# First layer's opening of a two-layer decoder trunk: row tiles side by side in fixed orders, products that nobody reads, and compression behind the first gates

## The chip, the cores and the metric

One Trainium2 chip, one core. The metric is device microseconds of one execution, median of several runs. The core has five engines that run their own instruction streams and wait for each other by semaphores: TensorE (PE, with its weight loads shown apart as PEld), VectorE (DVE), ScalarE (ACT), GpSimd (POOL) and SyncE (SP, which here issues the transfers from DRAM).

## The reference, cut to what matters

A sequence of 256 rows of width 1024 goes through two layers. Each layer normalises its rows, projects them, mixes them in two head groups (a gated linear recurrence and a block-sparse attention), and ends with a gated feed-forward block.

```
for l in range(DEPTH):                                  # 2 layers
    xn = rms_norm(h, norm_mix[l])                       # 256 x 1024
    proj = xn @ w_in[l]                                 # columns: hq hf hi hg | nq kc vc ksl vsl ksw vsw | gates
    o_hg = hgrn2_mixer(hq, hf, hi, hg, lb[l], hg_gnorm[l])
    o_nsa = nsa_mixer(nq, kc, vc, ksl, vsl, ksw, vsw, ngate, ...)
    h = h + concat(o_hg, o_nsa) @ w_out[l]
    xn = rms_norm(h, norm_ffn[l])
    h = h + (silu(g) * u) @ w_ffn_out[l]                # g, u = xn @ w_ffn_in[l]
# inside nsa_mixer: kc, vc = compress(...) = silu(blocks @ w1) @ w2, with w1 of 2048 x 256 for k and for v
```

## The kernel before

Rows are two tiles of 128 (t = 0, 1). Every float32 product is made of three: an operand is split into a high part (`whi`, `xh`; written by ScalarE as a copy in a shorter format) and a low part (`wlo`, `xl`; VectorE's difference), and `mm3` adds high·high, high·low and low·high in PSUM. So each weight piece ("unit", 512 KB, or 280 KB for the narrow block C) is loaded into one of 4 raw buffers (`wraw`), split by ScalarE (line 143) and VectorE (line 144) into one of 6 split buffers, and used by TensorE. A raw buffer is free when its unit is split; a split buffer is free when TensorE has used its unit for the last time.

The input projection runs in column blocks: B (4 units; keys and values of compression and of one attention branch), C (4 narrow units), A (4 units; the queries), then the gates: for the first pair of heads `hf` (2 units, PSUM tile `pf`) and `hq` (2 units, `pq`), later the same for the second pair. B, C and A are computed by `proj_tok` for row tile 0 over all four units and then for row tile 1, so a unit is held until row tile 1 has used it. `pf`, `pq` and the PSUM tiles of B and A (`pt`) share the two banks of tag "a" in turn: `pf` takes the bank in which A's row tile 0 stood.

Compression takes B's result: ScalarE copies it out (`kvc`, line 444), TensorE turns it (`pa`, line 458), VectorE writes `flat`; 64 narrow products with `w1` (8 loads of 512 KB, tile `w`, line 470) give `phid` (line 510), then `hid`, `phT`, `hk` and `hv`, `pkc`, and at last `kcb` and its transpose `pkT` (line 551).

A scheduler puts each engine's instructions in order when the program is built; on the chip each engine then takes its own list strictly in that order. `tc.high_priority` moves instructions ahead, and `after(a, b)` makes a stand behind b. Loads go out by SP's list in the same way. There are 8 transfer semaphores, used in turn, so SP issues a load only when the load 8 places earlier has landed.

The opening is `norm_T` for each row tile: squares (ScalarE), a power of -0.5 (GpSimd), scaling by the row's factor and the norm's weights (`xn`, VectorE, line 343), transposes (TensorE, line 346), and the split of the transposed rows (`x`, lines 351 and 352). The weights of the first norm are one row of 1024 numbers; `pgain` (line 250) spreads it over 128 partitions by a product with a row of ones.

Of the kernel before, what the change touches and what calls it, by code (L numbers as in the profile page):

```python
# [43 lines left out]
HOLD, HOLD_C = (18, 18, 16, 36), 1  # L44

# [45 lines left out]
def trunk(ctx: ExitStack, tc: tile.TileContext, x, w_in, w_out, lbl, gnorm, q_gain, k_gain,  # L91
# [19 lines left out]
    def unit(src, a, b):  # L111
        units.append([src, a, b, None, None, None, None])
        return len(units) - 1
# [19 lines left out]
    def split_to(n):  # L133
        while state["split"] < min(n, len(units)):
            load_to(state["split"] + 1)
            u = units[state["split"]]
            a, b = u[1], u[2]
            hi = wsp.tile([128, 1024], F32R, name="whi")
            lo = wsp.tile([128, 1024], F32R, name="wlo")
            u[4] = hi[:, : a * b].rearrange("p (a b) -> p a b", b=b)  # L140
            u[5] = lo[:, : a * b].rearrange("p (a b) -> p a b", b=b)
            with tc.high_priority(offset=SPLIT_PRIO):
                after(S.activation(u[4], u[3], AF.Copy), state.pop("behind", ()))  # L143
                u[6] = V.tensor_sub(u[5], u[3], u[4].bitcast(F32))  # L144
            state["split"] += 1
# [89 lines left out]
    ident = C("ident")  # L235
# [8 lines left out]
    nc.gpsimd.memset(mhalf, -0.5)  # L244
    ones = one.tile([128, 128], F32, name="ones")
    nc.gpsimd.memset(ones[0:1], 1.0)
# [11 lines left out]
    for hp in range(2):  # L258
        nc.gpsimd.memset(AT[hp], 0.0)

    kB = one.tile([128, 2, 2, T], F32R, name="kB")
    for g in range(2):
        nc.gpsimd.memset(kB[64 - 64 * g:128 - 64 * g, g].bitcast(F32), 0.0)
# [35 lines left out]
    def setup_tables():  # L299
        G = nc.gpsimd  # L300
        V.tensor_copy(idb, ident)
        V.tensor_copy(cab, tmp0[:, :128])
        V.tensor_copy(lev_m, tmp0[:, 128:208])
        for l in range(NL):
            gq = qk_g[:, 64 * l:64 * l + 64]
            ks = [qk_g[:, NL * 64 + 192 * l + 64 * b:NL * 64 + 192 * l + 64 * b + 64] for b in range(3)]
            for i, g in enumerate((gq, ks[1], ks[2])):
                gb = g[:, None, :].to_broadcast([128, NT, 64])
                G.tensor_mul(tabs[:, l, i, 0], cos, gb)
                for a in range(2):  # L310
                    s0, s1 = slice(32 * a, 32 * a + 32), slice(32 - 32 * a, 64 - 32 * a)
                    G.tensor_mul(tabs[:, l, i, 1, :, s0], sin[:, :, s0],
                                 g[:, None, s1].to_broadcast([128, NT, 32]))
                if i == 0:
                    G.tensor_scalar(tabs[:, l, i], tabs[:, l, i], 0.125, None, op0=OP.mult)
            G.tensor_mul(tabc[:32, l, 0], C("cosc", 32), ks[0][:32])
            for a in range(2):
                s0, s1 = slice(32 * a, 32 * a + 32), slice(32 - 32 * a, 64 - 32 * a)
                G.tensor_mul(tabc[:32, l, 1, s0], C("sinc", 32)[:, s0], ks[0][:32, s1])

# [8 lines left out]
    def norm_T(t, gain, xh, xl, tag, behind=(), hold=None):  # L329

        with tc.high_priority():
# [3 lines left out]
            for a in range(2):  # L335
                cs = slice(512 * a, 512 * a + 512)
                sq = S.activation(xn[:, cs], h[:, t, cs], AF.Square, scale=D ** -0.5, accum_out=ss[:, a:a + 1])
                after(sq, behind)
# [22 lines left out]
    for l in range(NL):  # L361
# [3 lines left out]
        last = [norm_T(0, gain0, *X[:2], "c", hold=end + HOLD[0] if l else None)[0]]  # L365
        if l == 0:
            norm_T(1, gain0, *X[:2], "c", last)
            setup_late()
            setup_tables()
# [69 lines left out]

        begin = len(products)  # L440
        for t, p in proj_tok("B"):
# [8 lines left out]

        flat = wk.tile([128, 2, 16, 32], F32, name="flat", tag="n4", bufs=3)
# [14 lines left out]
        w1t = []  # L466
        for u in range(4):
            w = wk.tile([128, 2, 4, 256], F32, name="w1", tag="big" if u < 3 else "turn", bufs=3 if u < 3 else 1)
            for i, w1 in enumerate((w1_k, w1_v)):
                DMA.dma_start(w[:, i], w1[l].rearrange("(j p) n -> p j n", p=128)[:, 4 * u:4 * u + 4])  # L470
            w1t.append(w)

# [25 lines left out]
        rs = rstd(ss, 24, 64, "qk_rs")  # L498
        gates(0)


        p = bank("phid", "e")[:, :256]
        for u in range(4):
# [539 lines left out]
```

## Time and profile before

| what | value |
|---|---|
| median of 3 runs | 684.99 us (684.43 to 685.22) |
| profiled execution, its own time | 685.0 us |
| its span (first to last instruction) | 683.1 us |
| TensorE busy | 667.0 us, 98% of the span |
| weight loads of TensorE busy | 554.6 us, 81% |
| VectorE busy | 469.7 us, 69% |
| ScalarE busy | 379.6 us, 56% |
| transfers | 118.9 MB, 174 GB/s on average |

Busy times of the engines overlap, so they don't add up. The time of an execution is 1.9 us more than its span. A share of TensorE near 100% says that it is seldom idle, not that it runs at its peak: a matmul that is slow counts as busy.

### The profile page before, as it was taken

Reading aid. Unit: us, or ns where it says so; the run is one execution under the profiler, and the core shown is the slowest. Engines: PE = TensorE matmul, PEld = TensorE weight load, DVE = VectorE, ACT = ScalarE, POOL = GpSimd, SP = SyncE. Lnnn points to the kernel's source line nnn. Section 1 sums busy time; section 2 is a strip of 40 time slices with the busy share of each in tenths; the row PEclk is TensorE's granted clock in tenths of the full one; section 3 lists DMA queues with packets and bytes.
Section 4 is the critical chain, followed back from the end, with each engine's and each line's share of the span. In section 5 each row is a group of like instructions: output and inputs, shape, how many; then the busy total and the mean of one; then the engine's idle time right before and its main releaser. Section 6 shows DMA issues by size and latency. Waiting matters only on the chain.

```text
span 683.1 us, 11845 instructions
## 1 busy us (share of the span) xinstructions
PE 667.0 (98%) x4607; PEld 554.6 (81%) x4607; DVE 469.7 (69%) x853; ACT 379.6 (56%) x676; POOL 30.1 (4%) x72
## 2 busy tenths in 40 slices
PE   6999999999999999999999999999999999999997
PEld 3869876688888888888878897658898888888886
DVE  4879999577665556666588979858685566665552
ACT  5536778636555555555466558656555555555550
POOL 2600001001000000000010000010000000000000
PEclk9999999999999999999999999999999999999999
DMA  7798541353765665666678632404376666665521
GB/s 253 246 335 266 169 107 51 100 178 121 248 187 187 190 192 194 194 185 185 196 230 286 203 110 64 125 1 154 94 229 203 188 187 190 197 191 187 185 93 62
DMA packets 86574, 118.90 MB, mean 174 GB/s; under 512 B 5035, under 2 KB 69365, under 8 KB 86518
## 3 DMA queue, kind: packets, MB, share of 16 engines
q1 hardware_dynamic: 86518, 118.15, 56.1%
q8 instruction: 36, 0.59, 0.4%
q14 instruction: 20, 0.16, 0.1%
HBM read 117.08 MB, written 1.05 MB: 173 GB/s over the span
## 4 chain that ended last, share of the span: by engine, by line
PE 80%; DVE 8%; DMA 4%; ACT 4%; issue 2%; POOL 1%; SPq 0%; POOLq 0%; DVEq 0%; ACTq 0%
PE pgu L929 22%; PE pz L327 17%; PE pgu L932 11%; PE pt L327 9%; PE py L327 5%; DMA wraw<-in_w_in_dram 4%; DVE wlo L144 3%; PE pO L673 2%; PE pgt L327 2%; ACT whi L143 2%; PE pPT L662 2%; PE pf L327 1%; PE pxn L346 1%; PE pl L779 1%; PE pq L327 1%
## 5 line engine op out<-in xcount | busy, mean ns | idle before, releaser
L144 DVE TENSOR_TENSOR wlo<-wraw,whi 128x1024 fp32r<-128x1024 f32 (+1 forms) x204 | 244.9, 1206 | 141.7 <-ACT whi L143 140.6
L143 ACT ACTIVATE whi<-wraw 128x1024 fp32r<-128x1024 f32 (+1 forms) x204 | 212.4, 1044 | 147.1 <-PE pgu L929 43.5
L929 PE MATMUL pgu<-x,whi 128*128 128x512 f32 x640 | 174.7, 394 | 0.0
L929 PEld LDWEIGHTS pgu<-x,whi 128*128 128x128 f32 x640 | 110.7, 189 | 15.7
L327 PE MATMUL pz<-whi,ahl 128*128 128x512 f32 x352 | 112.5, 391 | 0.0
L932 PEld LDWEIGHTS pgu<-x,wlo 128*128 128x128 f32 x640 | 98.1, 189 | 13.5
L932 PE MATMUL pgu<-x,wlo 128*128 128x256 f32 x640 | 101.7, 281 | 0.0
L327 PE MATMUL pt<-whi,x 128*128 128x512 f32 (+1 forms) x320 | 97.9, 383 | 0.0
L327 PEld LDWEIGHTS pz<-whi,ahl 128*128 128x128 f32 x352 | 65.9, 188 | 13.9 <-DVE ahl L946 0.5
L327 PE MATMUL pz<-wlo,ahl 128*128 128x512 f32 x176 | 68.9, 392 | 0.0
L327 PEld LDWEIGHTS pt<-whi,x 128*128 128x128 f32 x320 | 58.5, 191 | 10.3 <-DVE x L352 0.5
L327 PE MATMUL pt<-wlo,x 128*128 128x512 f32 (+1 forms) x160 | 61.6, 385 | 0.3 <-DVE wlo L144 0.3
L327 PE MATMUL py<-whi,x 128*128 128x512 f32 x128 | 42.0, 398 | 0.0
L327 PEld LDWEIGHTS pz<-wlo,ahl 128*128 128x128 f32 x176 | 33.0, 188 | 6.4
L327 PEld LDWEIGHTS pt<-wlo,x 128*128 128x128 f32 x160 | 30.6, 191 | 5.2 <-DVE wlo L144 0.7
L592 ACT ACTIVATE P<-pS,nm 128x128 f32<-128x128 f32 (+1 forms) x64 | 26.1, 424 | 6.3 <-DVE nm L639 5.0
L327 PEld LDWEIGHTS py<-whi,x 128*128 128x128 f32 x128 | 24.1, 188 | 4.7
L938 ACT ACTIVATE sl<-sl 128x512 f32<-128x512 f32 x20 | 12.7, 634 | 27.0 <-DVE sl L937 27.0
L327 PE MATMUL py<-wlo,x 128*128 128x512 f32 x64 | 25.1, 392 | 0.0
L327 PE MATMUL pf<-x,whi 128*128 128x256 f32 x128 | 23.8, 286 | 0.1
L327 PE MATMUL pgt<-whi,x 128*128 128x256 f32 x128 | 23.8, 285 | 0.0
L327 PE MATMUL pq<-x,whi 128*128 128x256 f32 x128 | 23.6, 284 | 0.0
(222 smaller groups left out, 829.4 us busy)
## 6 DMA issues: line engine op xcount, KB each, us to landing
wraw<-in_w_ffn_in_dram SPq DMA_DIRECT2D x88, 512.0 KB, 3.6
wraw<-in_w_in_dram SPq DMA_DIRECT2D x48, 512.0 KB, 5.3
wraw<-in_w_ffn_out_dram SPq DMA_DIRECT2D x44, 512.0 KB, 3.7
w<-in_cmp_w_k_dram SPq DMA_DIRECT2D x8, 512.0 KB, 4.7
w<-in_cmp_w_v_dram SPq DMA_DIRECT2D x8, 512.0 KB, 7.1
wraw<-in_w_out_dram SPq DMA_DIRECT2D x16, 256.0 KB, 4.1
wraw<-in_w_out_dram SPq DMA_DIRECT2D x8, 512.0 KB, 4.9
wraw<-in_w_in_dram SPq DMA_DIRECT2D x8, 280.0 KB, 5.3
```

The source lines that it names most:

```text
L143: after(S.activation(u[4], u[3], AF.Copy), state.pop("behind", ()))
L144: u[6] = V.tensor_sub(u[5], u[3], u[4].bitcast(F32))
L327: products.append(PE.matmul(o, a[u], b[v], start=start and i == 0, stop=stop and i == 2, skip_group_check=skip))
L346: tr = PE.transpose(p[:, 128 * k:128 * k + 128], xn[:, 512 * c + 128 * k:512 * c + 128 * k + 128], ident)
L592: e = S.activation(o, i, f, **kw)
L662: PE.transpose(p[:, 128 * hg:128 * hg + 128], P[t, g][:, hg, b, 128 * sb:128 * sb + 128], ident)
L673: m = PE.matmul(po[64 * g:64 * g + 64], vtok[:, b, sb, 64 * g:64 * g + 64], pts[g][0], start=(b == 0 and sb == 0), stop=False, skip_group_ ...
L779: m = PE.matmul(pl[32 * n:32 * n + 32, hp, 2 * t + i], K[:, i, ts], QF[:, i, ts].rearrange("p (n c a) -> p n c a", c=2, a=half)[:, :, 1], ...
L929: products.append(PE.matmul(pp[b], w[0][:, k, s], X[2][:, 4 * hh + k].rearrange("p c t -> p (c t)"), start=(hh == 0 and k == 0), stop=Fals ...
L932: products.append(PE.matmul(pp[b][:, T:], w[1][:, k, s], X[0][:, 4 * hh + k], start=False, stop=(hh == 1 and k == 3), skip_group_check=True))
L938: S.activation(sl, sl, AF.Silu)
```

## The change

The first layer's opening is written out by hand in `first_rows`, with the order of ScalarE, VectorE and GpSimd fixed by `after`. Block B of the first layer is computed by `proj_first`, with the two row tiles side by side unit by unit. The norm's weights go by ScalarE's queue into a row of a zeroed tile and are spread by products of 128 rows (`first` is a matrix with ones in its first row only). The identity matrix is made by GpSimd in place of a load. Seven bf16 products of 512 columns (`spin`), which nobody reads, stand at the head of TensorE's list. GpSimd's memsets and tables come behind the norms. The loads of `w1` and the products with it stand behind the first gates in the program, and `setup_late` and three casts stand later.

```diff
+SPIN = 7
     grow = wk.tile([128, D], F32, name="gain")
-    DMA.dma_start(grow[0:1], norm_mix[0:1])
+    cst = one.tile([128, NKEEP], F32, name="cst")
+    idle = one.tile([128, 512], BF16, name="idle")
+    V.memset(idle, 1.0)
+    V.memset(grow[:, :512], 0.0)
+    G.memset(ident, 1.0)
+    G.memset(grow[:, 512:], 0.0)
+    G.affine_select(ident, ident, pattern=[[-1, 128]], compare_op=OP.is_equal, fill=0.0, base=0, channel_multiplier=1)
...
+    last_pool = G.memset(first[0:1], 1.0)
+    S.dma_start(grow[0:1], norm_mix[0:1])
...
-    cst = one.tile([128, NKEEP], F32, name="cst")
-    DMA.dma_start(cst[:, :128], consts[:, :128])
...
+    def spin(n):
+        for _ in range(n):
+            PE.matmul(spin_bank, idle[:, :128], idle, start=True, stop=True)
+
+    spin(SPIN)
...
-        PE.matmul(gain0[a], ones[0:1], grow[0:1, 512 * a:512 * a + 512], start=True, stop=True)
+        PE.matmul(gain0[a], first, grow[:, 512 * a:512 * a + 512], start=True, stop=True)
...
+        with tc.high_priority():
+            squares(0)
+            normed(0, 0)
+            normed(0, 1)
+            split()
+            pv = turned(0, 0)
+            hi(0, 0, pv)
+            lo(0, 0, pv)
+            squares(1)
+            normed(1, 0)
+            split()
+            pv = turned(1, 0)
+            hi(1, 0, pv)
+            lo(1, 0, pv)
+            normed(1, 1)
...
+        def second(t):
+
+            with tc.high_priority():
+                pv = turned(t, 1, products[-1:])
+                hi(t, 1, pv)
+                lo(t, 1, pv)
+                split()
...
+        def proj_first(name):
+
+            ps_ = [bank("pt", "a") for _ in range(NT)]
+            for q, t in ((0, 0), (1, 0), (0, 1), (1, 1), (2, 0), (2, 1), (3, 0), (3, 1)):
...
-        for t, p in proj_tok("B"):
+        for t, p in proj_tok("B") if l else proj_first("B"):
...
-        w1t = []
-        for u in range(4):
-            w = wk.tile([128, 2, 4, 256], F32, name="w1", tag="big" if u < 3 else "turn", bufs=3 if u < 3 else 1)
...
         rs = rstd(ss, 24, 64, "qk_rs")
+        w1t = []
+        for u in range(4):
+            w = wk.tile([128, 2, 4, 256], F32, name="w1", tag="big" if u < 3 else "turn", bufs=3 if u < 3 else 1)
...
         gates(0)
+        if l == 0:
+            for o, i in ((idb, ident), (cab, tmp0[:, :128]), (lev_m, tmp0[:, 128:208])):
+                after(V.tensor_copy(o, i), [units[U["A", 3]][6]])
...
-                        PE.matmul(p[r0:r0 + 32], flat[:, kv, j], w[:, kv, 2 * jj + q],
-                                  start=(j < 2), stop=(j >= 14))
+                        with tc.high_priority(offset=BLOCK_PRIO):
+                            m = PE.matmul(p[r0:r0 + 32], flat[:, kv, j], w[:, kv, 2 * jj + q],
+                                          start=(j < 2), stop=(j >= 14))
+                        after(m, behind)
+                        behind = [m]
```

Three places in the lists of the built program matter for what follows.

SP's list at the loads of block C of the first layer (280 columns each), of `w1` (tile `w`) and of A (512 columns each). Before:

```order
L123 DMA wraw<-in_w_in_dram 128x2x280 x4
L470 DMA w_359<-in_cmp_w_k_dram 128x4x256
L123 DMA wraw<-in_w_in_dram 128x2x512 x4
L470 DMA w_359<-in_cmp_w_v_dram 128x4x256
L470 DMA w_362<-in_cmp_w_k_dram 128x4x256
```

Now, from the same place on:

```order
L124 DMA wraw<-in_w_in_dram 128x2x280 x2
L603 DMA w_573<-in_cmp_w_k_dram 128x4x256
L124 DMA wraw<-in_w_in_dram 128x2x280
L603 DMA w_573<-in_cmp_w_v_dram 128x4x256
L124 DMA wraw<-in_w_in_dram 128x2x280
L124 DMA wraw<-in_w_in_dram 128x2x512 x4
L124 DMA wraw<-in_w_in_dram 128x4x256 x2
L603 DMA w_576<-in_cmp_w_k_dram 128x4x256
```

One load of `w1` now stands ahead of C's third unit and two ahead of its fourth; the other six stand behind the first gates' first loads (4x256).

ScalarE's list from the end of block B of the first layer on: `kvc`, `sqk` and `vtok` take B's result from PSUM (`pt_225` and `pt_308` before, `pt_216` and `pt_217` now, row tiles 0 and 1), `whi` of 560 elements is the high part of a unit of C. Before:

```order
L444 ACTIVATE kvc_224<-pt_225 128x512
L425 ACTIVATE sqk_299<-pt_225 128x128
L447 ACTIVATE vtok_223<-pt_225 128x128
L291 ACTIVATE lbe_181<-lbe_181 128x8
L143 ACTIVATE whi_244<-wraw_242 128x560
L143 ACTIVATE whi_262<-wraw_248 128x560
L143 ACTIVATE whi_274<-wraw_250 128x560
L444 ACTIVATE kvc_224<-pt_308 128x512
L143 ACTIVATE whi_286<-wraw_252 128x560
```

Now:

```order
L144 ACTIVATE whi_266<-wraw_264 128x560
L144 ACTIVATE whi_272<-wraw_270 128x560
L144 ACTIVATE whi_278<-wraw_276 128x560
L549 ACTIVATE kvc_215<-pt_216 128x512
L516 ACTIVATE sqk_321<-pt_216 128x128
L552 ACTIVATE vtok_214<-pt_216 128x128
L144 ACTIVATE whi_302<-wraw_282 128x560
L549 ACTIVATE kvc_215<-pt_217 128x512
```

The copy of row tile 0 has moved behind the third unit of C, and that of row tile 1 behind the fourth.

VectorE's list at the end of block A of the first layer: `qn` and `qt` read A's row tiles from PSUM (`pt_467` is row tile 0, whose bank `pf` takes next; `pt_524` is row tile 1). Before:

```order
L488 TENSOR_REDUCE qk_ss_221<-sq_516 128x2x4
L492 TENSOR_TENSOR qn_466<-pt_467,tabs_121 128x2x4x64
L495 TENSOR_TENSOR qt_519<-pt_467,tabs_121 128x8x32 x2
L497 TENSOR_TENSOR qn_466<-qn_466,qt_519 128x2x4x64
L488 TENSOR_REDUCE qk_ss_221<-sq_549 128x2x4
```

Now:

```order
L592 TENSOR_TENSOR qn_466<-pt_467,tabs_136 128x2x4x64
L146 TENSOR_TENSOR wlo_493<-wraw_401,whi_492 128x1024
L146 TENSOR_TENSOR wlo_505<-wraw_413,whi_504 128x1024
L595 TENSOR_TENSOR qt_519<-pt_467,tabs_136 128x8x32
L146 TENSOR_TENSOR wlo_587<-wraw_472,whi_586 128x1024
L146 TENSOR_TENSOR wlo_617<-wraw_484,whi_616 128x1024
L595 TENSOR_TENSOR qt_519<-pt_467,tabs_136 128x8x32
```

Four low parts now stand between the first and the last reading of row tile 0: those of the two units of `hq` (`wlo_493`, `wlo_505`) and of the two units of the second pair's `hf` (`wlo_587`, `wlo_617`). With 6 split buffers these four take the buffers of A's four units. On TensorE's list `pf` follows A directly now, then `pq`, then the 64 products of compression; before, compression stood between A and `pf`. In the second layer the lists are the same as before, but for names.

## Rows read from the trace of the kernel before

**Rows 1.** The page's first line.

```profile
span 683.1 us, 11845 instructions
```

**Rows 2.** Stretches: us; PE, PEld, DVE, ACT, POOL busy (instructions); clock, DMA share, GB/s.

```profile
63.00:85.00 22.00, 20.76 (x207) 18.67 (x207) 20.35 (x47) 15.80 (x31) 0.00 (x0) 1.00 0.66 190
85.00:683.00 598.00, 590.80 (x4058) 491.02 (x4056) 403.51 (x714) 331.95 (x595) 13.94 (x30) 1.00 0.53 163
```

**Rows 3.** Timeline of the opening: start us, us, engine, instruction, idle time before it.

```profile
5.74 0.57 POOL L340 TENSOR_TENSOR n_ss<-n_ss,mhalf 128x1 f32<-128x1 f32 x1
...
8.48 1.23 DVE L144 TENSOR_TENSOR wlo<-wraw,whi 128x1024 fp32r<-128x1024 f32 x1 [2.73 <-ACT whi L143]
9.62 1.40 DVE L343 SCALAR_TENSOR_TENSOR xn<-h,n_ss,pgain 128x512 f32<-128x512 f32 x2
10.42 1.97 PE L346 MATMUL pxn<-cst,xn 128*128 128x128 f32 x8 [4.24 <-DVE xn L343]
...
12.81 0.63 PE L327 MATMUL pt<-wlo,x 128*128 128x512 f32 x1
14.10 0.63 PE L327 MATMUL pt<-wlo,x 128*128 128x512 f32 x1
...
17.21 0.39 PE L327 MATMUL pt<-wlo,x 128*128 128x512 f32 x1
17.90 0.39 PE L327 MATMUL pt<-wlo,x 128*128 128x512 f32 x1
```

**Rows 4.** Timeline of SP's queue, with the issues of loads.

```profile
0.72 0.35 SPq L206 DMA_DIRECT2D gain<-in_norm_mix_dram  x1
2.00 0.43 SPq L210 DMA_DIRECT2D cst<-in_consts_dram  x1
...
15.94 1.92 SPq L123 DMA_DIRECT2D wraw<-in_w_in_dram  x4
...
26.29 4.18 SPq L123 DMA_DIRECT2D wraw<-in_w_in_dram  x4
```

**Rows 5.** Stretches of 1 us, columns as in the second group.

```profile
22.00:23.00 1.00, 1.00 (x6) 0.82 (x5) 1.00 (x7) 1.00 (x3) 1.00 (x5) 1.00 1.08 384
23.00:24.00 1.00, 1.00 (x6) 0.83 (x5) 1.00 (x2) 0.70 (x2) 1.00 (x3) 1.00 0.63 222
```

**Rows 6.** Timeline of blocks C and A of the first layer.

```profile
26.39 0.60 ACT L444 ACTIVATE kvc<-pt 128x512 f32<-128x512 f32 x1 [2.69 <-PE pt L327]
26.89 0.66 ACT L143 ACTIVATE whi<-wraw 128x560 fp32r<-128x560 f32 x1
27.04 0.87 PE L458 MATMUL pa<-cst,kvc 128*128 128x128 f32 x6
30.13 0.40 PE L327 MATMUL pt<-wlo,x 128*128 128x280 f32 x1 [0.27 <-DVE wlo L144]
35.56 0.19 PEld L327 LDWEIGHTS pt<-wlo,x 128*128 128x128 f32 x1 [0.23 <-DVE wlo L144]
45.08 3.65 PE L510 MATMUL phid<-w,flat 128*32 128x256 f32 x62
```

**Rows 7.** Timeline of the first gates: third product of pf, last of pq, second pair's first.

```profile
50.84 0.37 PE L327 MATMUL pf<-x,wlo 128*128 128x256 f32 x1
62.07 0.28 PE L327 MATMUL pq<-x,wlo 128*128 128x256 f32 x1
63.00 0.48 PE L327 MATMUL pf<-x,whi 128*128 128x256 f32 x2
```

**Rows 8.** Timeline of the second layer, end of block A.

```profile
378.55 1.07 ACT L143 ACTIVATE whi<-wraw 128x1024 fp32r<-128x1024 f32 x1 [0.30 <-PE pt L327]
378.67 2.36 DVE L144 TENSOR_TENSOR wlo<-wraw,whi 128x1024 fp32r<-128x1024 f32 x2
382.14 0.42 DVE L495 TENSOR_TENSOR qt<-pt,tabs 128x256 f32<-128x256 f32 x1
```

**Rows 9.** Waits of TensorE from 12 to 90 us: us in total, times, longest.

```profile
PE pkT L551 <- DVE kcb L549: 0.8, 1, 0.8
```

More of the change, by code (lines that the diff above doesn't have):

```diff
@@ L243, in trunk @@
     mhalf = one.tile([128, 1], F32, name="mhalf")
-    nc.gpsimd.memset(mhalf, -0.5)
-    ones = one.tile([128, 128], F32, name="ones")
-    nc.gpsimd.memset(ones[0:1], 1.0)
+    mh = G.memset(mhalf, -0.5)
+    after(last_pool, [mh])
+    spin_bank = bank("pspin", "e")
+    def spin(n):
+        for _ in range(n):
+            PE.matmul(spin_bank, idle[:, :128], idle, start=True, stop=True)
+    spin(SPIN)
     gain0 = []
@@ L299, in setup_tables, with then @@
     def setup_tables():
[L300 to L303, printed above, removed]
+        def then(ins):
+            after(ins, pool_order[-1:])
+            pool_order.append(ins)
+        for hp in range(2):
+            then(G.memset(AT[hp], 0.0))
+        for g in range(2):
+            then(G.memset(kB[64 - 64 * g:128 - 64 * g, g].bitcast(F32), 0.0))
         for l in range(NL):
@@ L327, in mm3, with first_rows, then, split @@
             products.append(PE.matmul(o, a[u], b[v], start=start and i == 0, stop=stop and i == 2, skip_group_check=skip))
-    def norm_T(t, gain, xh, xl, tag, behind=(), hold=None):
+    pool_order = []
+    def first_rows(xh, xl):
+        xn, rs, order = [], [], {V: [], S: [], G: [last_pool]}
+        def then(eng, ins):
+            after(ins, order[eng][-1:])
+            order[eng].append(ins)
+        def split():
+            i = state["split"]
+            split_to(i + 1)
+            then(S, units[i][7])
+            then(V, units[i][6])
+        def normed(t, c):
+            cs = slice(512 * c, 512 * c + 512)
+            then(V, V.scalar_tensor_tensor(xn[t][:, cs], h[:, t, cs], rs[t], gain0[c], op0=OP.mult, op1=OP.mult))
+        def turned(t, c, behind=()):
+            p = bank("pxn", "c")
+            for k in range(4):
+                cs = slice(512 * c + 128 * k, 512 * c + 128 * k + 128)
+                after(PE.transpose(p[:, 128 * k:128 * k + 128], xn[t][:, cs], ident), behind)
+            return p.rearrange("p (k t) -> p k t", t=128)
+        def hi(t, c, pv):
+            dh = xh[:, 4 * c:4 * c + 4, 128 * t:128 * t + 128]
+            then(S, S.activation(dh, pv, AF.Copy))
+        def lo(t, c, pv):
+            sl = slice(4 * c, 4 * c + 4), slice(128 * t, 128 * t + 128)
+            then(V, V.tensor_sub(xl[:, sl[0], sl[1]], pv, xh[:, sl[0], sl[1]].bitcast(F32)))
+        def squares(t):
+            ss = sm.tile([128, 4], F32, name="n_ss")
+            xn.append(wk.tile([128, D], F32, name="xn", tag="vs", bufs=2))
+            for a in range(2):
+                cs = slice(512 * a, 512 * a + 512)
+                then(S, S.activation(xn[t][:, cs], h[:, t, cs], AF.Square, scale=D ** -0.5,
+                                     accum_out=ss[:, a:a + 1]))
+            then(G, G.tensor_scalar(ss[:, 2:3], ss[:, 0:1], ss[:, 1:2], EPS, op0=OP.add, op1=OP.add))
+            then(G, G.tensor_tensor(ss[:, 3:4], ss[:, 2:3], mhalf, op=OP.pow))
+            rs.append(ss[:, 3:4])
+        with tc.high_priority():
[19 more added lines that the diff above has]
+                split()
+        pool_order.extend(order[G])
+        return second
@@ L331, in norm_T @@
+    def norm_T(t, gain, xh, xl, tag, hold=None):
         with tc.high_priority():
@@ L364, in trunk @@
         X = xT()
[L365 to L368, printed above, removed]
+        if l:
+            norm_T(0, gain0, *X[:2], "c", hold=end + HOLD[0])
+        else:
+            second = first_rows(*X[:2])
             setup_tables()
```

49 lines of the change are left out of this document (30 added, 19 removed).

## Prediction

> **What bounds the kernel now.** I read the windows by stage first, because a busy share says nothing of a stage. TensorE is busy for 590.8 of the last 598 us and for 20.8 of 22 us between 63 and 85 us [rows 2]. The change leaves the number of products the same but for a few, so it can gain only where TensorE waits: at the start, in a few short stalls, and in the 1.24 us it stands idle between 63 and 85 us. The profiled execution took 685.0 us for its span of 683.1 us [rows 1], which is also the median, 684.99; the sum below is made against 685.0.
>
> Next came the timeline of the opening. The row's factor is ready when GpSimd's `n_ss` ends at 5.74 + 0.57 = 6.31 us, but `xn` starts at 9.62: on VectorE it stands behind the first low part (8.48 us, 1.23 us long). TensorE is idle for 4.24 us until the first transposes at 10.42 [rows 3]. Its products then come three in 1.29 us (0.43 each, from 12.81 to 14.10), and later three in 0.69 us (0.23 each, from 17.21 to 17.90): the lower level of the clock, 1.2 GHz, first, and 2.4 GHz later [rows 3].
>
> Third, SP's queue and the transfers. Loads arrive at 384 GB/s up to 23 us, and at 222 GB/s in the microsecond after that [rows 5]; so the queue runs dry at about 23 + 222/384 = 23.6 us, and the last load in it is the first of `w1`, issued behind C's four [rows 4].
>
> Fourth, the timeline of blocks C and A. `kvc` of row tile 1 ends at 26.99 and `pa` follows at 27.04. Products of C wait twice for low parts, 0.27 and 0.23 us, and A ends at 45.08, where `phid` begins [rows 6]. From there to the second pair's first product at 63.00 TensorE has 96 products of the first gates and compression [rows 7].
>
> **Step 1: the opening ends block B earlier.** `xn` now stands ahead of the first low part, and SP issues two loads fewer ahead of the first weights, 0.35 + 0.43 = 0.78 us [rows 4]. So `xn` can start at about 6 us. VectorE's list to the end of B is then 4 scalings of 0.70 (1.40 for two), 4 low parts of 1.23 and 4 low parts of turned rows, with as many elements as `xn`, taken at 0.70 [rows 3]: 10.5 us. From 6 us that is 16.5; four turns of four transposes that VectorE waits for, 1.97 us for eight [rows 3] and so 1 us each, partly beside its work, taken at 0.7, make 19.3, and the last unit's 12 products at 0.23 make 22. Before, row tile 1's copy waited on block B until 26.39 [rows 6]. The four microseconds are not the gain, since what follows waits for something else.
>
> **Step 2: `w1` and C share the queue.** SP's list has one `w1` load ahead of C's third unit and two ahead of the fourth. A load of 512 KB is 1.37 us at 384 GB/s [rows 5]. C's fourth unit was the last but one, at 23.6 - 1.37 = 22.2; now it is the last, so it lands at 23.6, less 0.78 for the earlier issues and 0.17 for the identity matrix (64 KB) that is no longer loaded, plus 1.37 for the second `w1` load: 23.9. ScalarE takes its list in order: high part of C's fourth unit (0.66), `kvc` of row tile 1 (0.60), then `pa` [rows 6]. With 0.1 at the start and at each of two hand-offs that is 23.9 + 0.66 + 0.60 + 0.3 = 25.5, against 27.04: **-1.5 us**. Its bounds: if the loads land in another order and C is not held back, B's end binds, and `pa` comes at 22 + 0.66 + 0.60 + 0.1 = 23.4 (-3.6); if both `w1` loads cost C their full time and ScalarE's other copies too, the gain is 0.2.
>
> **Step 3: C and A.** With everything split earlier the two stalls go, 0.27 + 0.23 [rows 6]; a product more between is 0.13. So **-0.4**, and A ends at 45.08 - 1.9 = 43.2.
>
> **Step 4: a wait that was not there.** `pf` now follows A directly and takes the bank of A's row tile 0. It can start only when VectorE has read that bank for the last time, and the last `qt` stands behind four low parts. The last of these is of a unit whose split buffer was that of A's last unit, free only when A is over. So behind A's end come a high part, a low part and `qt` one after the other, with TensorE idle. Layer 2 shows the same hand-over, where nobody waits for it: the high part starts at 378.55 (0.30 us after ScalarE went idle for it) and takes 1.07, and two low parts end at 381.03 [rows 8], 2.5 us after the high part began. With 0.42 for `qt`, 0.2 from A's end to the high part and 0.2 for the way to TensorE it is **+3.3**. Lower bound: 0.1 + 1.07 + 1.18 + 0.42 + 0.1 = 2.85, one low part alone. Upper bound: 4.8, if VectorE is late as a whole. Nothing else is in front of TensorE in its list, so nothing covers the wait. Before, compression stood there, 3.65 us of `phid` [rows 6], and covered it.
>
> **Step 5: from A's end to the second pair.** Before: 63.00 - 45.08 = 17.9 us. The first gates are 94 products from 50.84 to 62.07 [rows 7], 0.12 each; 96 make 11.5. Of `phid` 62 products took 3.65 [rows 6], 64 make 3.8. So 2.6 us were turns and waits. In the new order compression comes after `pq`, its inputs long ready, and the other six `w1` loads are issued behind the first gates' loads. Those are needed from about 58 us; at the 190 GB/s of the stretch behind [rows 2] they take 16 us from 34 us on, so the work of A and of the first gates hides them (each one late would cost up to 1.4). I take 1.75 us for the turns and one remaining wait: **-0.85** (0 to -1.2).
>
> **Step 6: behind 63 us.** Idle are 1.24 us [rows 2], of which `pkT` waits 0.8 for VectorE [rows 9]. That wait has the same neighbours and should stay; of the rest I take **-0.5** (-1.2 to +0.7, because scan and attention up to 85 us are interleaved anew).
>
> The other edits (identity by GpSimd, memsets behind the norms, three late casts, two more table loads of ScalarE) cost nothing: ScalarE is busy 15.8 of 22 us, GpSimd not at all [rows 2]. Without that cover they would cost a microsecond or two. Unread products can only raise the clock earlier; since B's end doesn't bind, at most the 0.5 us by which B would end later without it.
>
> Sum: 685.0 - 1.5 - 0.4 + 3.3 - 0.85 - 0.5 = **685.0**. The saving at the opening goes into the wait for `pf`'s bank.
>
> **The rivals.**
> *No hold-up by `w1`* (faster). Several loads are in flight at once and the later may land first. For it: SP issues C's four in 1.92 us, faster than they land [rows 4]. Against it: the stretch is at its highest rate, so bytes ahead delay bytes behind [rows 5]. Step 2 gives 2.1 more: 682.9.
>
> *The clock falls* (slower). In the 3.3 us wait TensorE is idle, and may start again at 1.2 GHz. After the idle start it was active from 10.42 on, still slow at 14.10 and fast at 17.21 [rows 3]: 3.7 to 6.8 us at 0.43 for 0.23, a loss of 1.7 to 3.2 us. With 2.7 the time is 687.7; it decides from about 1.4 us of loss. For it: the wait is nearly as long as the 4.24 us before the slow start. Against it: TensorE is never idle as long once warm, so no row shows a fall. The Trainium skill, "TensorE: Matmul & The Clock Gate", section "🎯 Why this matters for your kernels", advises against gaps without matmuls between bursts, since the clock falls back; by that rule the wait would end at 1.2 GHz, and the time would be the 687.7 just given. Nothing in before tests it.
>
> *VectorE is late* (slower). It is busy 20.35 of 22 us behind 63 us [rows 2]. If low parts, `flat` and the scaling of queries pile up, step 4 goes to its upper bound and step 6 to no gain: 685.0 + 1.2 + 0.5 = 686.7.
>
> *The change doesn't do what it says.* If the unread products leave the clock low, B ends at 23 rather than 22, and `pa` moves by less than 0.5: 685.4, inside the forecast.
>
> **How the numbers follow.** No change 0.42, with its own range 683.7 to 686.4; `w1` no hold-up 0.25; clock 0.12; VectorE late 0.13; 0.08 for a larger part of step 6 (683.4). This kernel's measurement tells 0.2%, 1.4 us, from no change. So faster 0.25 + 0.08 = 0.33, same 0.42, slower 0.25. The range 682.4 to 687.8 takes in both near cases and half of the clock's; below it and above it I leave about 1 in 10 each.
>
> **What the profile after would show.** Step 1: `xn` at about 6, first product before 9, B's end at 22. Step 2: the high part of C's fourth unit at 24, `pa` at 25.5; at 23.4 the first rival is right. Step 3: A ends at 43.2. Step 4: TensorE idle for 3.3 us ahead of `pf`, released by VectorE's `qt`; if it is below 1 us, the sum is wrong by two and the kernel is faster. Products of `pf` that take twice 0.12 show the clock rival. Step 5: the second pair at 63.5. Step 6: idle between 63 and 85 us under 1.24. The prediction would be wrong if `pf` finds its bank free, if `w1` lands late, or if new waits stand behind 63 us.

## The result, and the profile after

| | before | after |
|---|---|---|
| median, us | 685.11 (684.43 to 685.59, 4 runs) | 691.57 (689.72 to 692.75, 4 runs) |
| profiled execution, its own time, us | 685.0 | 692.2 |
| its span, us | 683.1 | 690.2 |
| TensorE busy, us | 667.0 | 668.5 |

The change makes the kernel slower: ratio 1.0093, with a 95% interval of 1.0067 to 1.0118. That is 6.5 us where the forecast was no change, and above the forecast's range (to 687.8).

The timeline of the opening after the change answers to [rows 3].

```profile
5.84 0.30 POOL L390 TENSOR_SCALAR n_ss<-n_ss 128x1 f32<-128x1 f32 x1 [3.65 <-ACT xn L388]
6.82 1.40 DVE L366 SCALAR_TENSOR_TENSOR xn<-h,n_ss,pgain 128x512 f32<-128x512 f32 x2 [4.83 <-POOL n_ss L391]
9.08 0.73 PE L539 MATMUL pt<-whi,x 128*128 128x512 f32 x2 [0.80 <-ACT x L377]
22.94 0.23 PE L298 MATMUL prow<-ident,tmp 74*128 74x74 f32 x1
```

The same product of B in the kernel before:

```profile
12.22 0.79 PE L327 MATMUL pt<-whi,x 128*128 128x512 f32 x1
```

`xn` now starts when its factor is ready, the first product of B comes 3.1 us earlier, and the last row follows B's last product: B ends at about 23.0, 3 us earlier than before. So far the opening does what it says. What becomes of the 3 us is in the waits of TensorE from 12 to 100 us (us in total, times, longest):

```profile
PE pa L565 <- ACT kvc L549: 4.3, 2, 2.8
PE pf L346 <- DVE qt L595: 2.8, 1, 2.8
```

and, for the first of them, in SP's queue (start, length of the issue) and ScalarE's list, which answer to [rows 4] and [rows 6].

```profile
11.46 0.35 SPq L237 DMA_DIRECT2D qk_g<-in_q_gain_dram  x1
12.80 0.35 SPq L238 DMA_DIRECT2D qk_g<-in_k_gain_dram  x1
...
16.13 0.88 SPq L124 DMA_DIRECT2D wraw<-in_w_in_dram  x2
17.06 0.53 SPq L603 DMA_DIRECT2D w<-in_cmp_w_k_dram  x1
17.69 1.16 SPq L124 DMA_DIRECT2D wraw<-in_w_in_dram  x1
18.90 0.52 SPq L603 DMA_DIRECT2D w<-in_cmp_w_v_dram  x1
```
```profile
24.81 0.67 ACT L144 ACTIVATE whi<-wraw 128x560 fp32r<-128x560 f32 x1 [1.63 <-DMA wraw<-in_w_in_dram]
25.39 0.58 ACT L549 ACTIVATE kvc<-pt 128x512 f32<-128x512 f32 x1
26.02 0.44 PE L565 MATMUL pa<-ident,kvc 128*128 128x128 f32 x2 [2.85 <-ACT kvc L549]
27.05 0.67 ACT L144 ACTIVATE whi<-wraw 128x560 fp32r<-128x560 f32 x1 [0.75 <-DMA wraw<-in_w_in_dram]
27.62 0.58 ACT L549 ACTIVATE kvc<-pt 128x512 f32<-128x512 f32 x1
28.26 1.44 PE L565 MATMUL pa<-ident,kvc 128*128 128x128 f32 x6 [1.40 <-ACT kvc L549]
```

B has been ready since 23.0. But each copy of it stands behind a high part of C, and each of these waits for its load. TensorE waits 2.85 and 1.40 us. Block C's first load is issued at 16.13, no earlier than before (15.94). C's third and fourth load are issued later than before, at 17.69 and 19.51 instead of 16.93 and 17.44: they need buffers that VectorE's low parts of B set free, and with `xn` ahead these come later. What this alone costs here is not shown, since the queue moves 376 GB/s from 20.0 to 23.2 us anyway. B's third and fourth low part, before and after:

```profile
13.15 1.23 DVE L144 TENSOR_TENSOR wlo<-wraw,whi 128x1024 fp32r<-128x1024 f32 x1 [0.21 <-ACT whi L143]
15.19 1.22 DVE L144 TENSOR_TENSOR wlo<-wraw,whi 128x1024 fp32r<-128x1024 f32 x1
```
```profile
16.05 1.23 DVE L146 TENSOR_TENSOR wlo<-wraw,whi 128x1024 fp32r<-128x1024 f32 x1 [0.26 <-ACT whi L144]
17.88 1.36 DVE L146 TENSOR_TENSOR wlo<-wraw,whi 128x1024 fp32r<-128x1024 f32 x1
```

The windows by stage show what follows (core 0: us, then busy us and instructions of PE, PEld, DVE, ACT and POOL, the granted clock PEclk, the DMA share, GB/s):

```profile
23.20:28.20 5.00, 0.83 (x5) 0.60 (x5) 2.74 (x8) 2.64 (x7) 4.91 (x11) 1.00 1.07 372
28.20:32.00 3.80, 3.74 (x18) 3.75 (x19) 3.80 (x12) 3.51 (x6) 1.83 (x5) 0.55 0.86 274
47.30:50.25 2.95, 0.12 (x1) 0.03 (x1) 2.95 (x5) 1.54 (x2) 0.00 (x0) 1.00 1.05 341
```

TensorE is busy for 0.83 of the first 5.0 us. In the 3.8 us behind them its granted clock is 0.55, so nearly all of it is at the lower level: `pa` takes 1.44 us where it took 0.87, and eleven products of C come at 0.23 us instead of 0.13, some 1.6 us together. A ends at 47.26 instead of 45.08. Then TensorE stands idle again, for the bank of `pf`, which follows the last `qt` (timeline; VectorE is never idle here):

```profile
47.02 0.42 DVE L595 TENSOR_TENSOR qt<-pt,tabs 128x256 f32<-128x256 f32 x1
47.36 2.42 DVE L146 TENSOR_TENSOR wlo<-wraw,whi 128x1024 fp32r<-128x1024 f32 x2
49.69 0.42 DVE L595 TENSOR_TENSOR qt<-pt,tabs 128x256 f32<-128x256 f32 x1
50.25 0.48 PE L346 MATMUL pf<-x,whi 128*128 128x256 f32 x2 [2.83 <-DVE qt L595]
```

The difference of the two spans, 7.1 us, by three places that stand in both timelines: A's end (47.26 and 45.08) +2.2; from there to the feed-forward block's first product, tile `pgt` (164.26 and 159.83), +2.2; from there to the end (525.9 and 523.3) +2.7.

### The profile page after: what moved, and what is told of

Read it like the earlier page. It is cut to its first block, busy times and chain, and to the rows that moved or that the text cites. A ratio compares the mean times of both kernels' runs of the same rounds, so it can differ in the third digit from the quotient of the medians.

```text
span 690.2 us, 11872 instructions
## 1 busy us (share of the span) xinstructions
PE 668.5 (97%) x4614; PEld 554.0 (80%) x4614; DVE 469.4 (68%) x855; ACT 382.2 (55%) x678; POOL 33.0 (5%) x76
## 4 chain that ended last, share of the span: by engine, by line
PE 83%; DVE 5%; ACT 4%; DMA 4%; issue 1%; POOL 1%; SPq 0%; POOLq 0%; DVEq 0%; ACTq 0%
PE pgu L1042 21%; PE pz L346 17%; PE pgu L1045 11%; PE pt L346 10%; PE py L346 6%; DMA wraw<-in_w_in_dram 3%; PE pf L346 3%; PE pO L786 3%; DVE wlo L146 2%; PE pq L346 2%; ACT whi L144 2%; PE pPT L775 1%; PE pgt L346 1%; PE phid L621 1%; PE pl L892 1%
## 5 line engine op out<-in xcount | busy, mean ns | idle before, releaser
L346 PE MATMUL pt<-whi,x 128*128 128x512 f32 (+1 forms) x288 | 87.8, 381 | 0.0
L346 PEld LDWEIGHTS pt<-whi,x 128*128 128x128 f32 x288 | 52.5, 192 | 7.9 <-DVE x L443 0.2
L346 PE MATMUL pt<-wlo,x 128*128 128x512 f32 (+1 forms) x144 | 54.4, 378 | 0.0
L346 PEld LDWEIGHTS pt<-wlo,x 128*128 128x128 f32 x144 | 27.7, 192 | 3.8
L346 PEld LDWEIGHTS pf<-x,whi 128*128 128x128 f32 x128 | 20.1, 191 | 4.1 <-issue 4.0
```

What stands on the lines that cost most here:

```text
L346: products.append(PE.matmul(o, a[u], b[v], start=start and i == 0, stop=stop and i == 2, skip_group_check=skip))
```

## Experiments

Times are medians; in brackets the ratio to the kernel before, timed beside it (684.9 to 685.1), with its interval. "Changed" is the changed kernel, 691.6. A's end is where the next product can follow A's last one, as in the 47.26 and 45.08 above.

**w1_behind.** All loads of `w1` behind C's four.

```diff
-                DMA.dma_start(w[:, i], w1[l]...)
+                ld = DMA.dma_start(w[:, i], w1[l]...)
+                if l == 0:
+                    after(ld, [units[U["C", 3]][8]])     # the load of C's fourth unit
```

> All loads of w1 stand behind C's four in SP's list; TensorE's list is unchanged. Theory 1 (C's loads are late because w1's share the queue, and ScalarE's copies of B stand behind C's high parts): C's fourth high part starts at about 23 us instead of 27.05, TensorE's waits for kvc fall from 4.25 us to about 1, the products of C behind them no longer come at 0.23 us, A ends about 4.5 us earlier than 47.26, and the time is about 687.1, 4.5 below the changed kernel. Rival (SP's issue is paced by other loads, so C is late whatever stands ahead): C's fourth high part at 25 or later, gain 1 us or less, 690.6. Second rival (VectorE's low parts take over as the bound of block A): waits for kvc vanish, but A gains less than 2.5 us.

Measured: 691.56 [1.0083 to 1.0118]. C's fourth high part started at 24.01 instead of 27.05, and A ended at 44.7, 2.6 us earlier. The wait for `kvc` fell to 0.2 us; a part of that is that B itself ended late in this execution, at 24.8 (in w1_qt, with the same lists up to here and B's end at 23.0, it is 1.1). The gain at A's end is far from the 4.5 us of my theory and lies just above the second rival's mark of 2.5. C's third and fourth load were issued at 19.33 and 21.06, the latter when B's fourth low part had ended (21.04), so here it is VectorE's later list and no longer `w1` that sets their date. Nothing of the gain is left in the time: the wait for `pf`'s bank grew, `pf` started 1.8 us earlier, at 48.4, and then ran at the lower clock.

```profile
PE pf L346 <- DVE qt L595: 3.6, 1, 3.6
PE pt L346 <- DVE wlo L146: 0.9, 1, 0.9
```
```profile
48.00:50.00 2.00, 1.56 (x7) 1.59 (x8) 2.00 (x4) 0.06 (x1) 0.00 (x0) 0.50 1.07 345
50.00:52.00 2.00, 2.00 (x12) 2.00 (x11) 2.00 (x7) 0.00 (x0) 0.00 (x0) 0.50 1.09 351
52.00:54.00 2.00, 2.00 (x11) 2.00 (x11) 0.70 (x2) 0.27 (x1) 0.00 (x0) 0.50 1.09 351
```

Eleven or twelve products in 2 us where eighteen or nineteen come at the full clock: `pf` took 8.6 us instead of 6.0. The low part that A waited for 0.9 us was late because VectorE stood idle for GpSimd:

```profile
30.07 0.65 DVE L571 TENSOR_TENSOR flat<-pa,vecs 64x480 f32<-64x480 f32 x1 [3.12 <-POOL flat L559]
```

**kvc_first.** ScalarE's copies of B ahead of C's third and fourth high part.

```diff
+            if l == 0:
+                after(units[U["C", 2 + t]][7], [cp])     # cp is the copy kvc of row tile t
```

> ScalarE copies B's row tile 0 ahead of the high part of C's third unit and row tile 1 ahead of the fourth; the loads stand as in the changed kernel and TensorE's list is unchanged. Theory 1 (it is ScalarE's order that makes TensorE wait, the late loads alone cost little): pa starts at about 24.0 instead of 26.02 and 28.25, one wait of about 0.7 us for the low part of C's fourth unit is left, C ends at about 32.4 instead of 36.5, time about 687.7, 3.9 below the changed kernel. Rival (the loads of C bind by themselves): TensorE waits for C's low parts what it no longer waits for kvc, gain below 1.5 us, 690 or more.

Measured: 693.0 [1.0102 to 1.0137], 1.4 us above the changed kernel in the medians, with intervals that overlap. The wait for `kvc` fell to 1.8 us, the clock did not fall behind it, and A ended at 43.4. `pf` started at 49.5 all the same, behind a wait of 5.9 us and at the lower clock. A part of that wait is not A's: in this kernel the scheduler has put three low parts of VectorE (from 44.64) ahead of both last readings of row tile 0 (`qn` at 48.04, `qt` at 48.64). Both my theory and its rival had the price at the wrong place.

**qt_first.** VectorE's last reading of A's row tile 0 ahead of the four low parts.

```diff
+                if l == 0 and t == 0 and a == 1:
+                    for i in range(U["A", 3] + 3, U["A", 3] + 7):
+                        after(units[i][6], [tm])         # tm is the last qt of row tile 0
```

> VectorE's last reading of A's row tile 0 stands ahead of the four low parts; ScalarE swaps one high part, TensorE's list is unchanged. Theory 1 (the wait of 2.83 us ahead of the first gates is the order on VectorE, and nothing binds behind it): the wait falls to below 0.5 us and the time is about 688.8, 2.8 below the changed kernel; the waits for kvc stay at 4.25 us. Rival (the low parts are then late for hq's products, pq, or for compression): a wait of 1 to 3 us appears ahead of pq or of the second pair's pf, and the time is within 1 us of the changed kernel.

Measured: 690.26 [1.0054 to 1.0097]. `pf` started at 46.9, with A's end; 1.0 us came back ahead of `pq`, which takes the bank of row tile 1 (released by VectorE too). The second pair started at 63.4 instead of 65.5. In the medians 1.3 us of the 2.8 are left, with intervals that overlap.

**clock_fill.** Nineteen unread products in the first of the two waits.

```diff
+                            for _ in range(19):
+                                m = PE.matmul(spin_bank, idle[:, :128], idle, start=True, stop=True)
+                                after(m, [last])
```

> Nineteen more unread products of 512 columns (0.22 us each at the higher clock, 4.2 in all) stand on TensorE between B's last product and pa, which now comes in one piece; the waits for the loads and copies stay. Theory 1 (the idle 4.25 us let the clock fall, and C's first products at 0.23 instead of 0.13 us cost 1.3 to 1.5): granted clock 1.00 throughout 26 to 32 us, C's products at 0.13, time about 690.2. Rival (the slow stretch has another cause, or its loss is made up behind it): products at 0.23 all the same, or the time stays at 691.6.

Measured: 692.76 [1.0100 to 1.0149]. The clock stayed at 1.00 from 24 to 32 us, and C's products came at 0.13: the slow stretch does follow from the idle time. The other profiles agree: behind waits for `kvc` of 3.1 to 4.3 us in two pieces (qt_first, phid_back, flat_only, changed) the clock fell, behind 1.1 to 1.8 us (w1_qt, w1_qt_flat_l2, nospin, kvc_first) it did not. But in this execution B ended at about 25.5 and the added products, four microseconds of them, held `pa` until 29.70. A ended at 47.7. So the price of the fall can't be read from the time of this run; 1.6 us stays worked out from the rows.

**w1_qt and w1_qt_flat.** Both mends together; then also GpSimd's memset of `flat` ahead of the second layer's tables (other lists unchanged).

```diff
         fm = nc.gpsimd.memset(flat, 0.0)
+        if l == 0:
+            after(state["table"], [fm])                  # the first table of layer 2
```

> Both mends at once: w1's loads behind C's four, and VectorE's last reading of A's row tile 0 ahead of four low parts. Theory 2 (w1_behind gained 2.4 us at A's end, and lost it again because the wait for pf's bank grew to 3.6 us and pf then ran at 1.2 GHz): with the bank free in time A ends at about 44.9, pf follows at once at 0.12 us a product, a wait of 1 to 1.5 us is left ahead of pq for the last reading of A's row tile 1, and the time is about 688.3. Rival (whatever is mended ahead of 50 us, a transfer or VectorE gives it back before the second pair): second pair's first product at 65 or later, time 690 or more.

> As w1_qt, and GpSimd's memset of flat stands ahead of the second layer's tables; the lists of the other engines are unchanged. Theory 2 (in w1_behind VectorE stood idle for 3.1 us behind GpSimd's memset of flat, and A's low parts were late by it): VectorE has no such wait, the 0.9 us that TensorE waited for a low part in block A vanish, time about 1 us under w1_qt, 687.3. Rival (that idle time of VectorE was slack): within 0.4 us of w1_qt.

Measured: w1_qt 690.13 [1.0059 to 1.0093], w1_qt_flat 687.37 [1.0023 to 1.0048]. In w1_qt VectorE waited 3.55 us for the memset, `pq` waited 3.0 us and then ran at 1.2 GHz; the rival was right, the second pair came at 66.2. With the memset ahead A ended at 43.5 and the second pair started at 61.5, 1.5 us earlier than in the kernel before [rows 7], but with work behind that start that the kernel before does ahead of it (see mended). The mend was worth 2.8 us, more than expected. **flat_only**, the same edit in the changed kernel:

> The changed kernel with GpSimd's memset of flat ahead of the second layer's tables; all other lists are unchanged. Theory 3 (in the changed kernel block C is so late that flat is not waited for; the memset binds only once C is mended): 691.6 within 0.8 us. Rival (GpSimd's late memsets are a part of the loss): 689 to 690.

Measured: 691.67 [1.0082 to 1.0109]. So the late memset is no part of the 6.5 us by itself; it becomes the bound when C is mended.

**phid_back and comp_move.** The two halves: the new opening with the loads of `w1` and the products at their old places in the program, and the old opening with both behind the first gates.

```diff
+        w1t = []                                         # comp_move: from ahead of block C to here
+        for u in range(4):
...
+                        with tc.high_priority(offset=BLOCK_PRIO):
+                            m = PE.matmul(p[r0:r0 + 32], flat[:, kv, j], w[:, kv, 2 * jj + q], ...)
+                        after(m, behind)
```

> The changed kernel with w1's loads and the products with w1 at their old places (between A and pf); the opening as changed. Theory 2 (the opening's orders alone cost the waits for kvc with the clock, and the move of compression the wait for pf's bank): waits for kvc 3 to 4.3 us stay, the wait for pf's bank is covered by 3.7 us of phid, time about 690, 1.5 under the changed kernel and 5 over before. Rival (the loss is the move's): 685 to 686.

> The kernel before with only the move: w1's loads and the products with w1 behind the first gates. C's four loads stay ahead of w1's, the opening is the old one. Theory 2: pa at 27.0 as before, A ends at about 45, TensorE then waits about 3 us for pf's bank, with a fall of the clock if it is idle as long as in w1_behind (2.6 us more); compression after the gates gives 0.8 back and scan and attention lose 1.1: time 687 to 691. Rival (the move is free by itself, the loss needs the new opening): 684.5 to 685.5.

Measured: phid_back 685.67 [0.9999 to 1.0023], comp_move 685.00 [0.9994 to 1.0012]. The rival was right in both: either half is free within the intervals, which end 0.2% and 0.1% above the kernel before, and the loss needs both. In phid_back TensorE waits 3.7 us for `kvc`, the clock falls, A ends at 47.0, all as in the changed kernel. But there the scheduler has put VectorE's last `qt` of row tile 0 ahead of the low parts, ten products with `w1` stand among `pf`'s first, and no wait for the bank is seen; the second pair starts at 63.0, as before the change. From A's end to the second pair it takes 15.9 us, before 17.9. Of these 2.0 us, 0.6 is idle time that is gone, and 1.3 are the products of `phT` and `pkc`, which here stand behind the second pair's first products; from there to `pgt` it takes 96.5 us all the same (before 96.8). In comp_move C's four loads stand ahead of `w1`'s, A ends at 45.8, and the wait for the bank is 1.2 us: here only three low parts stand ahead of the last `qt`.

**nospin.** The changed kernel without unread products (`SPIN = 0`).

> The changed kernel without the seven unread products; all other lists are unchanged. Theory 2 (block B's end doesn't bind, since ScalarE's copies wait for C's loads): the spreading products and the first products of B run at 0.43 us instead of 0.22 and B ends 1.5 to 2.5 us later, the wait for kvc is shorter by as much, pa starts where it did (26.0 and 28.2), time 691.6 within 1 us; if the shorter wait no longer lets the clock fall, 1 to 1.5 us less. Rival (the unread products carry the opening): 693 or more.

Measured: 690.33 [1.0064 to 1.0099], inside the expectation and, by its interval, not told from the changed kernel. The two parts of `pa` started at 25.2 and 27.4, 0.8 earlier than expected, the waits for `kvc` were 1.7 us, the clock did not fall behind them, A ended at 44.8, and the wait for `pf`'s bank was 3.5 us. So the unread products bring nothing that is seen here.

**before_l2.** The kernel before, with the second layer's copy `kvc` of row tile 1 ahead of the high part of A's second unit.

```diff
+            if l and t:
+                after(units[U["A", 1]][7], [cp])
```

> The kernel before, where in the second layer the copy kvc of row tile 1 stands ahead of the high part of A's second unit on ScalarE. Theory 2 (that copy, queued behind a high part whose load is late, is a wait of its own in the second layer: 0.4 us in the profile of before, 1.0 to 1.6 in most of the others): the wait ahead of pa in the second layer vanishes, 0.4 to 1 us less, 684.0 to 684.6. Rival (the low part of that unit binds at once): 685.0.

Measured: 684.19 [0.9982 to 1.0003]. The second layer has the hold-up of step 2 in both kernels. After the change (ScalarE and TensorE, profiled execution):

```profile
366.55 1.06 ACT L144 ACTIVATE whi<-wraw 128x1024 fp32r<-128x1024 f32 x1 [1.62 <-DMA wraw<-in_w_in_dram]
367.51 0.58 ACT L549 ACTIVATE kvc<-pt 128x512 f32<-128x512 f32 x1
368.14 0.87 PE L565 MATMUL pa<-ident,kvc 128*128 128x128 f32 x6 [1.54 <-ACT kvc L549]
```

and before:

```profile
361.94 0.87 PE L458 MATMUL pa<-cst,kvc 128*128 128x128 f32 x6 [0.36 <-ACT kvc L444]
```

In the profiles of the six kernels with this edit the stretch from `pgt` to the end took 523.2 to 523.6 us; in the twelve without it 523.3 (before) to 526.3, and 525.9 in the changed kernel's. So of the last 2.7 us of the difference 1.1 are this wait (1.5 and 0.4 us), which the change doesn't touch and which came out short in the profile of before; w1_qt_flat and w1_qt_flat_l2, which differ by this edit alone, take 525.22 and 523.46, so up to 1.8 us. The rest is not traced, and the edit was not run in the changed kernel alone.

**mended, mended_back, w1_qt_flat_l2.** mended is w1_qt_flat with the edit of before_l2, the loads of `w2` and of the next norm's weights behind C's, and the first norm's weights as SP's first load again; mended_back is that with `w1` at its old place; w1_qt_flat_l2 has the edit of before_l2 alone.

```diff
+            if state["loaded"] == 7:                     # C's fourth load
+                for ld in late:                          # w2, next norm's weights
+                    after(ld, [u[8]])
```

> w1_qt_flat and three more mends: the loads of w2 and of the next norm's weights behind C's four, so that C's first load is issued at about 13.6 instead of 16.1; the first norm's weights as first load by SP and spread by a product of one row, as before the change; the copy kvc ahead of A's second high part in the second layer. Theory 2 (transfers pace 16 to 52 us, and begin late): B ends at 23 or earlier, A at about 42.5, the second pair starts at about 60, the second layer's wait for kvc vanishes, time about 684.7. Rival (earlier loads gain nothing, VectorE paces): second pair's start at 61.5 as in w1_qt_flat, time 686.5 or more.

> As mended, with w1's loads and the products with w1 between A and pf again. Theory 2 (the opening gains once its copies and loads are not held up, and phid covers what pf waits for): second pair at 61.5 instead of 63.0, scan and attention as in before, time 683.0 to 683.8, under both kernels. Rival (w1's eight loads, now needed at 43 us, are late): phid waits, the second pair starts at 63 as in before, time 684.5 to 685.5.

> w1_qt_flat with the second layer's copy kvc of row tile 1 ahead of the high part of A's second unit. Theory 3 (that copy costs 1 to 1.6 us in most executions): wait ahead of pa in the second layer below 0.3 us, time 686.0 to 686.4, the rest of mended's gain by earlier loads. Rival (the gain was all by earlier loads and the opening): 687.4.

Measured: mended 685.07 [0.9990 to 1.0012], w1_qt_flat_l2 686.61 [1.0013 to 1.0031], mended_back 688.76 [1.0036 to 1.0064]. In mended the long waits ahead of 100 us are gone:

```profile
PE pS L760 <- issue: 0.7, 1, 0.7
PE pt L353 <- DVE wlo L150: 0.6, 2, 0.4
PE pq L353 <- DVE qt L608: 0.4, 1, 0.4
PE pa L578 <- ACT kvc L556: 0.4, 1, 0.4
```

and with them the whole loss, but the kernel is no faster than before: its second pair starts 2.4 us earlier, at 60.6, and `pgt` at 159.9, where it was. That start is mostly moved work. A ended at 44.8, only 0.3 us earlier than before, and behind the second pair's first product there now stand

```profile
61.51 1.06 PE L641 MATMUL phid<-w,flat 128*32 128x256 f32 x12 [0.20 <-DMA w<-in_cmp_w_v_dram]
63.07 0.63 PE L649 MATMUL phT<-cst,hid 128*128 128x64 f32 x4
65.24 0.61 PE L663 MATMUL pkc<-w,hv 128*128 128x64 f32 x4
```

and more of `pkc`, all of which the kernel before does ahead of it. From the second pair's start to `pgt` TensorE is busy for 98.3 us instead of 95.4 and idle for 1.0 instead of 1.4. Of the 2.3 us in the medians between w1_qt_flat and mended the second layer's copy gives 0.8, less than I expected; the rest came with the other two edits, which were not run apart. mended_back missed: in its profiled execution the clock was at 0.50 to 0.70 from 8 to 16 us and again at 52 to 56, behind a wait of 2.0 us for a low part.

**comp_qt and comp_qt_late.** comp_move with the edits of qt_first and before_l2; then also with the late loads of mended.

> comp_move (old opening, compression behind the first gates) with VectorE's last reading of A's row tile 0 ahead of the low parts and the second layer's copy kvc first. Theory 3 (comp_move still waits 1.2 us for pf's bank, and the second layer 0.4 to 1 us): second pair at 61.2 to 61.6 instead of 62.4, time 683.0 to 683.8, faster than both kernels. Rival (the time is set behind the gates, by scan and attention): 684.2 to 685.0.

> comp_qt with the loads of w2 and of the next norm's weights behind C's four. Theory 3 (in the old opening block B's end, not C's loads, decides when C starts, so that only A's and the gates' loads come earlier): within 0.5 us of comp_qt, or up to 1 us faster. Rival (w2's loads or the others are then late for compression): slower by 0.5 us or more.

Measured: comp_qt 684.76 [0.9987 to 1.0005], comp_qt_late 685.95 [1.0002 to 1.0024]. `pf` followed A at once in both, and the second pair started at 62.4 as in comp_move: 0.8 us of the gain went into a wait of `phid` for a load of `w1`, in comp_qt_late 1.8 us into one ahead of `pq`, and the clock fell behind it. No version was clearly faster than the kernel before.

## Why the prediction was wrong

**Step 1** was right, a little early: `xn` at 6.82 (forecast 6), first product at 9.08 (before 9), B's end at 23.0 (22). It varies: with the same opening B ended at 22.7 to 23.3 in most of the profiles, at 24.8 in w1_behind and w1_qt_flat and at about 25.5 in clock_fill.

**Step 2 failed, by its sign.** The second part of `pa` came at 28.26, not at 25.5: +1.2 us where the sum has -1.5, outside the bounds. I had seen both halves of the mechanism, the loads of `w1` ahead of C's and the copies behind C's high parts, but I dated C from the old end of the queue less 0.95 us for an earlier start. C's loads are not issued earlier: SP gets to them at 16.13 us, since from 8.8 to 12.8 us it issues one small load per 1.34 us and then five more, whatever the opening saved ahead of them. That is 1.5 of the 3.1 us by which the fourth high part is late (27.05, not 23.9), 0.55 of it in C's first load, which took 5.6 us to land instead of 5.2. Another 1.2 us is the date that I started from: before, C's fourth load landed at 23.4 and not at 22.2, as its row in the view of loads says (KB, us from issue to landing), with the issue at 17.44:

```profile
wraw<-in_w_in_dram SPq DMA_DIRECT2D x1, 280.0 KB, 6.0
```

The last 0.3 us is in the two loads of `w1` in between, 1.5 us each between landings for my 1.37. And I charged no clock to the wait. The rival *the clock falls* was there in this wait, not in the one where I looked, for about 1.6 us. w1_behind, w1_qt, clock_fill and nospin show the two causes: with `w1` behind C the fourth high part starts 3 us earlier and the wait shrinks to 0.2 to 1.1 us, and without the idle time the clock stays up.

**Step 3**: the two stalls went, as forecast, but A ended at 47.26 instead of 43.2. A's end is 4.1 us off; steps 4 and 5 together take 2.0 of that back, and step 6 is 5.1 off: together the 7.1 us between the forecast, no change, and the profiled spans.

**Step 4** was right in mechanism and near in size: 2.83 us for 3.3, released by `qt`. But I took it as a fixed price behind A's end. It isn't: when A ended earlier, in w1_behind and kvc_first, the wait grew to 3.6 and 5.9 us, and `pf` started between 48.4 and 50.3 in all these kernels. What ends last there is VectorE's list, which the rival *VectorE is late* names. An earlier A, on which my rival *no hold-up by `w1`* at 682.9 rests, gained nothing in these two kernels: in w1_behind `pf` started 1.8 us earlier, and at the lower clock it took 2.6 us longer.

**Step 5** gained more than forecast: the second pair started 18.3 us after A's end, where the forecast has 20.3 and before 17.9 [rows 6, 7]. A part of that is only moved: `phT` and `pkc` now stand behind its first products.

**Step 6**: idle time between 60 and 85 us fell from 1.24 to 0.39. But from the second pair's start on the sum has -0.5, and measured is a loss of 4.6: 1.9 up to `pgt` and 2.7 behind it. The 1.9 is work and not waiting: TensorE is busy for 97.5 us of that stretch instead of 95.4 and idle for 1.2 instead of 1.4. 1.3 us of it are `phT` and `pkc`, which step 5's gain has moved here; the other 0.8 is not traced. Of the 2.7, 1.1 to 1.8 are the second layer's `kvc`, which no part of the change moves and which I had not read as a risk. With the edit of before_l2 the kernels' medians moved by 0.8 to 0.9 only, so not all of the 2.7 belongs to the change's 6.5 us, and the rest of it is open.

**The other edits.** GpSimd's late memset of `flat` costs nothing in the changed kernel (flat_only), but 2.8 us once C is mended (w1_qt to w1_qt_flat). The cover that I named for it, ScalarE's and GpSimd's idle time behind 63 us, was not the one that mattered.

In mended there is little saving to take back, since its earlier second pair is mostly moved work. Left open is the rest: from the second pair's start to `pgt` the orders differ, 96.5 to 96.8 us with the products of `w1` at their old place (before, before_l2, phid_back, mended_back), 97.4 to 97.8 in comp_move, comp_qt and comp_qt_late and 98.4 to 99.3 in the others, so that this start can't be compared between them; no run took that apart.

## What to carry to other kernels

A copy that TensorE needs must not be queued behind work that waits for a load: it then costs the load's lateness, whoever caused it, and it differs from run to run. Date a load from its own issue and landing in the profile, not from when the queue runs dry, and ask what its issue waits for, the buffer that it fills included. Two edits that are free by themselves may cost together, here 6.5 us; time the halves before the whole.

## What was not expected of the hardware

TensorE's clock fell from the higher to the lower level in the middle of the kernel, and waits of the same length had both outcomes. Behind the wait for `pf`'s bank it stayed up after 2.83 us (changed kernel) and 3.5 us (nospin), and fell after 2.8 us (flat_only) and 3.6 us (w1_behind); in comp_qt_late it fell after 1.8 us ahead of `pq`. The Trainium skill, "TensorE: Matmul & The Clock Gate", section "🎯 Why this matters for your kernels", warns of gaps between bursts; these runs agree that the falls come behind gaps. The length of a single gap does not sort them here. The profile shows no fall in the opening: from 12 to 16 us of the kernel before, the granted clock reads 1.00, though products take 0.43 us each there and 0.23 from 17.2 us on. So the slow start that the rival *the clock falls* was priced from is read from the products' times alone. A fall cost 2.6 us over the 48 products of `pf` in w1_behind, as much again as the wait.

The opening's spreading of the norm's weights also came out in two ways: its four products took 1.96 us from 4.59 in the changed kernel and 3.75 us from 5.87 in w1_behind, where nothing ahead of them differs. In nospin, flat_only, qt_first and w1_qt_flat the profile shows them waiting for the weights' load, which ScalarE's queue issues at 2.1 us behind the rows and the first weights; in the changed kernel and in w1_behind it shows no such wait, so there the cause is not shown.
